# The compressed branch's probability product on 128 rows of the array instead of 64

## The chip, the cores and the metric

The kernel runs on one core of a Trainium2 chip. The metric is the device time of one execution in microseconds (us). The engines are PE (TensorE; its weight loads are listed apart as PEld), DVE (VectorE), ACT (ScalarE), POOL (GpSimd) and SP, which issues the DMAs. The kernel before took 587.68 us, the median of three runs (586.27, 587.68 and 588.92).

## The reference

Two layers of a decoder trunk on 512 tokens of 1024 channels. Each layer projects its input, runs three mixers side by side (retention, sparse attention, a gated linear recurrence), gates their outputs, projects them back and normalises. The change lies in the sparse attention, in the branch over compressed keys and values. Cut to that branch:

```python
kc = compress(kvh(k_c), cmp_pos[0], cmp_w[0])      # 31 compressed keys per group of heads
vc = compress(kvh(v_c), cmp_pos[1], cmp_w[1])      # 31 compressed values, 64 wide
p_c = masked_softmax(einsum('bgrqd,bgnd->bgrqn', qb, kc), m_c)
o_c = einsum('bgrqn,bgnd->bgrqd', p_c, vc)         # the product that is changed
o_s, o_w = ...                                     # selected blocks, sliding window
return gb[..., 0:1] * o_c + gb[..., 1:2] * o_s + gb[..., 2:3] * o_w
```

Two groups of four heads each share keys and values.

## The kernel before, in words

Every float32 product is made of two parts in the type float32r: a rounded high part and the rest as a low part. An operation of the program is not issued when it is written down. It is recorded as an `Op` (`Engine.__getattr__`, all under line 204) with a cost and its dependencies, and `Plan.schedule` then makes one fixed order per engine: a list schedule by the longest path to the end, to which a random number per operation is added (`noise[op.ix]`, 300 ns times a normal draw, `op.ix` being the operation's place in the program), and six rounds of packing backward and forward. `Plan.forward` gives each engine the operation that can start first. So the order on every engine, and which projection products stand between two steps of the attention, come from that plan; at run time the engines only wait on semaphores.

The attention (lines 983 to 990) runs, in each layer, over four tiles of 128 tokens in the order 1, 2, 0, 3 and over two groups. `scores` makes the probabilities, `softmax_cmp` those of the compressed branch (`pcm`, 4 heads by 32 columns). `values` adds all branches up in one PSUM bank `po` (tag `O`, one bank): for the other branches 128-row products of `vst` with the transposed probabilities `th` and `tl` (512 columns each), and at lines 964 to 973 the compressed branch. There `pcm` is transposed into a bank of tag `T`, four ACT copies put the high parts of the four heads on partitions 0 to 31 of `pc`, four DVE subtractions put the low parts on partitions 32 to 63, and one product of 512 columns with the stationary operand `vcs` closes the step. `vcs` holds the compressed values twice, on partitions 0 to 31 and 32 to 63, and their low parts in its second 64 columns; partitions 64 to 127 of both tiles exist and are not used. This product is made 16 times: 2 layers, 4 tiles, 2 groups. I call these the 16 sites.

`pc` has one place (`PCB = 1`), so each use waits until the product before has read it. `vcs` is written once per layer, by four small copies and subtractions at lines 709 to 712, and has one place as well. Projection products (bank tag `A`), retention (tag `M`), transposes (tag `T`) and scores (tag `S`) fill PE between the sites; nearly all of them use 128 rows and 128 columns. POOL works mainly on the low parts of the weights (`wl`), which the products of the next weights wait for.

Of the kernel before, what the change touches and what calls it, by code (L numbers as in the profile page):

```python
# [10 lines left out]
F32 = mybir.dt.float32  # L11
F32R = mybir.dt.float32r
# [5 lines left out]
P = 128  # L18
# [17 lines left out]
# columns of w_in in the order in which they are projected  # L36
# [36 lines left out]
# columns of the table of constants  # L73
# [38 lines left out]
COLD = 6827.0  # the array's clock is halved until then  # L112
TURN = 130.0  # between two engines' accesses to a bank
GRAIN = 8
# [4 lines left out]
PCB = 1  # L119
# how a token tile's halves are normalised: on DVE; on ACT and DVE; on ACT, DVE and Pool  # L120
# [16 lines left out]
class Ref:  # L137
    """A view of a buffer whose place is known once the schedule is."""
# [26 lines left out]
class Slots:  # L165
    """Places of one kind; buffers take them in the order in which they are made."""
# [23 lines left out]
class Engine:  # L190
# [23 lines left out]
    def locks(self, what, args, kw):  # L214
        """Whether an instruction holds the SBUF ports that DVE and Pool share."""
        at = lambda x: x.view(0) if isinstance(x, Ref) else x
        if self.name == "POOL":
            return True
        if self.name != "DVE":
            return False  # L220
        big = [at(x) for x in args[1:] if isinstance(x, Ref) and int(np.prod(at(x).shape[1:])) > 1]
        big += [at(v) for k, v in kw.items() if isinstance(v, Ref) and k not in ("accum_out", "scalar1", "scalar2")]
        sbuf = [x for x in big if x.space != PSUM]
        if len(sbuf) > 1:
            return True
        return what in ("tensor_copy", "tensor_scalar", "memset") and len(sbuf) == len(big) and at(args[0]).space != PSUM

    def together(self, *products):
        """Matrix products that the array takes side by side, as one instruction of the plan."""
        def call():  # L230
            for out, lhsT, rhs, kw in products:
                self.queue.matmul(out.view(), lhsT.view(), rhs.view(), **kw)  # L232

        cost = self.cost("matmul", products[0][:3], {}) + 102.0 * (len(products) - 1)
        self.plan.add(self.name, call, cost, [r for x in products for r in x[1:3]], [x[0] for x in products], None, False)
# [35 lines left out]
class Plan:  # L271
# [7 lines left out]
    def touched(self, ref):  # L279
        """The quarters of the partitions and the cells of GRAIN elements that a view touches, as bits."""  # L280
        ap = ref.view(0)
        key = (tuple(map(tuple, ap.ap)), ap.offset, ap.space == PSUM)
        if key not in self.cells:
            (stride, count), *free = key[0]
            first, at = divmod(ap.offset, stride)
            cells = np.array([at])
            for st, n in free:
                cells = np.unique((cells[:, None] + st * np.arange(n)).ravel())
            if ap.space == PSUM:
                cells = np.arange(512)  # L290
                first, count = 0, P
            rows = sum(1 << q for q in range(first // 32, (first + count - 1) // 32 + 1))
            self.cells[key] = rows, sum(1 << int(c) for c in np.unique(cells // GRAIN))
        return self.cells[key]
# [34 lines left out]
    def schedule(self):  # L329
        """A list schedule by the longest path to the end, then rounds of packing to the end and to the start."""  # L330
        rank, noise = {}, NOISE * np.random.RandomState(SEED).standard_normal(len(self.ops))
        for op in reversed(self.ops):
            rank[op] = op.cost + max((self.lag(op, o) + rank[o] for o in op.before), default=0.0)
        self.end = self.forward({op: noise[op.ix] - rank[op] - op.bias for op in self.ops})
        best = self.end, {op: op.start for op in self.ops}
        for _ in range(ROUNDS):
            self.end = self.forward(self.backward())
            if self.end < best[0]:
                best = self.end, {op: op.start for op in self.ops}
        if best[0] < self.end:  # L340
            self.end = self.forward(best[1])
        return self.end

    def forward(self, prio):
        """Every engine takes what it can start first, the least prio first; the end of the last."""
# [13 lines left out]
        def place(op):  # L359
            """When the buffers that an instruction is the first to touch have places, or None."""  # L360
            t = 0.0
            for b in op.bufs:
                if b.slot is None:
                    if b.pool.next != b.at or not b.pool.free:
                        return None
                    t = max(t, min(b.pool.free)[0])
                t = max([t] + [end + TURN for e, end in b.seen.items() if e != op.eng])
            return t
# [45 lines left out]
    def backward(self):  # L414
        """The latest starts that still end with the last schedule, with its places for the buffers."""
# [19 lines left out]
        start = {}  # L435
# [28 lines left out]
def hybrid_kernel(ctx: ExitStack, tc: tile.TileContext, xt_d, xn_d, w_in_d, w_out_d, gb_d, cmpw_d, cmpp_d, lruw_d,  # L464
# [29 lines left out]
    # products of zeros, which raise the array's clock while the first loads are on their way  # L494
# [5 lines left out]
    # x, later y, transposed, as two float32r parts  # L500
# [8 lines left out]
    # ---------------------------------------------------------------- weights  # L509
# [9 lines left out]
    def weights(l, name):  # L519
        if (l, name) not in parts:  # L520
# [5 lines left out]
            for h in W_HALVES:  # L526
# [4 lines left out]
                if first:  # L531
                    # a slice of the weights and of x at a time
# [23 lines left out]
    def proj_t(w, m, out):  # L556
        """out [128 columns m of the chunk, 512 tokens] = W^T X^T"""
        c = slice(m * P, (m + 1) * P)
        for n, k in enumerate(K_ORDER):
            hi, lo = w[k]  # L560
            T.matmul(out, hi[:, c], XH[:, k, :], start=(n == 0), stop=False)
            T.matmul(out, hi[:, c], XL[:, k, :], start=False, stop=False)
            T.matmul(out, lo[:, c], XH[:, k, :], start=False, stop=(n == KT - 1))

    def proj_n(w, tiles, order=K_ORDER):
        """out [128 tokens of tile i, columns of the chunk] = X W for each (i, out)"""
# [9 lines left out]
    for l in range(DEPTH):  # L576
        last = l == DEPTH - 1
        # ------------------------------------------ values and branch gates
# [19 lines left out]
        # ------------------------------------------ parameters  # L598
# [13 lines left out]
        # log-decay of the LRU: sp = softplus(-lam), c1 = -4 sp, c2 = 2 sp  # L612
# [23 lines left out]
        # ------------------------------------------ keys, two stacked parts  # L636
        # per group and part: the selected keys, last tile first; the compressed keys; the window's keys
# [20 lines left out]
        # ------------------------------------------ queries, two stacked parts  # L658
# [16 lines left out]
        # ------------------------------------------ compressed keys and values  # L675
        vcs = sb([P, 2, 2 * HD], "vcs", dt=F32R)
        w = weights(l, "cmp")
# [9 lines left out]
        # keys and values side by side in the array's columns  # L687
# [4 lines left out]
        for i in range(2):  # L692
# [9 lines left out]
            else:  # L702
                # twice over the partitions, for the two parts of the probabilities
# [11 lines left out]
        # ------------------------------------------ retention  # L715
# [37 lines left out]
        def retention():  # L753
            for n in range(NT):
# [5 lines left out]
                # queries of two heads on the partitions; keys of one head, the other head's rows zero  # L760
# [58 lines left out]
        # ------------------------------------------ RG-LRU  # L819
        def lru():  # L820
# [14 lines left out]
            for c in range(2):  # L835
# [4 lines left out]
                for e in range(2):  # L840
                    # a block's two parts over each other, its two gates side by side
# [29 lines left out]
        # ------------------------------------------ attention  # L871
        def gate_rec(d, i, g, b):
            """d <- 0.25 gate / d"""
# [10 lines left out]
        def softmax(i, g, b, r, ps, p_, d, nmx):  # L884
            """exp(score - max) of one head and branch, and its sum"""
# [6 lines left out]
        def softmax_cmp(i, g, pcm):  # L892
            """the compressed branch's probabilities from its masked scores, four heads"""
# [10 lines left out]
        def scores(i, g, branches):  # L904
            """the scaled probabilities of the branches: 0 selected (tiles in falling order), 1 window"""
# [18 lines left out]
            for r in range(4):  # L924
                tile_ = sb([P, S], "P", PBUFS)
                # columns of kst for each bank, and what lies where in it
# [24 lines left out]
        def values(i, g, probs, pcm, po, first, last):  # L951
# [12 lines left out]
            if pcm is not None:  # L964
                # the high parts over the low parts
                pt = bank("T")
                T.transpose(pt[:, :P], pcm.rearrange("p r n -> p (r n)"), ident)
                pc = sb([P, 4, P], "pc", PCB, F32R)
# [4 lines left out]
                T.matmul(po, vcs[0:64, g, :], pc[0:64].rearrange("p r t -> p (r t)"), start=False, stop=last)  # L973
# [20 lines left out]
        # ------------------------------------------ gates of the NSA output  # L994
# [30 lines left out]
        # ------------------------------------------ output projection, norm  # L1025
# [66 lines left out]
def _layout(inputs):  # L1092
# [14 lines left out]
    # per block of channels: its weights twice over the partitions; columns of the two gates, the block's own half first  # L1107
# [28 lines left out]
```

## Time and profile before

| | before |
|---|---|
| median of 3 runs | 587.68 us (586.27 to 588.92) |
| span of the profiled execution | 586.1 us |
| PE busy | 564.7 us, 96% |
| weight loads (PEld) busy | 498.3 us, 85% |
| DVE / ACT / POOL busy | 71% / 57% / 50% |
| granted TensorE clock, mean | 0.995 of full speed |

The profile is of one execution. For it only the span from the first to the last instruction is known; it lies 0.2 us under the fastest of the three runs and 1.6 us under their median. Matmuls are pipelined and the ends in their rows are modelled, so that neighbouring matmuls overlap in the rows. What one product takes of PE's time is read from start to start, not from its length.

### The profile page before, as it was taken

What the parts mean: (1) busy time and instruction counts of PE and PEld (TensorE: products, weight loads), DVE (VectorE), ACT (ScalarE), POOL (GpSimd) and SP (SyncE); (2) the same over time, 40 slices, a digit from 0 to 9 for tenths busy, and PEclk for the clock granted to TensorE, in tenths of its full rate; (3) what the DMA queues carried; (4) which work ended last, traced back from release to release, by engine and by line L of the source; (5) the groups of instructions that cost most, each with busy time, mean ns of one, the idle gap of its engine ahead of it and who ended that gap; (6) DMA issues with size and microseconds to landing.
All of it is one profiled execution on the core that took longest, in us unless ns stands there. A gap on an engine that the chain in (4) does not pass through costs nothing.

```text
span 586.1 us, 10490 instructions
## 1 busy us (share of the span) xinstructions
PE 564.7 (96%) x3670; PEld 498.3 (85%) x3670; DVE 415.7 (71%) x1237; ACT 336.7 (57%) x785; POOL 294.6 (50%) x349
## 2 busy tenths in 40 slices
PE   8999999999989999999989999999999999999994
PEld 8888867889878888899988888788899888788994
DVE  6663499889998776743793227798797888676247
ACT  6464477698666655722443456758985666564220
POOL 3655155335845255754483454432596514378532
PEclk9999999999999999999999999999999999999997
DMA  8733222110323044343362433120213202332403
GB/s 259 263 100 108 73 72 73 38 36 1 85 61 91 4 124 116 100 148 104 137 180 55 125 79 103 37 73 1 73 38 107 71 21 57 106 127 59 134 7 145
DMA packets 44069, 52.63 MB, mean 90 GB/s; under 512 B 2928, under 2 KB 36720, under 8 KB 44016
## 3 DMA queue, kind: packets, MB, share of 16 engines
q1 hardware_dynamic: 44016, 51.95, 29.8%
q8 instruction: 29, 0.48, 0.3%
q14 instruction: 24, 0.20, 0.1%
HBM read 47.75 MB, written 4.19 MB: 89 GB/s over the span
## 4 chain that ended last, share of the span: by engine, by line
PE 71%; DVE 14%; ACT 8%; issue 2%; DMA 2%; POOL 2%; SPq 0%; DVEq 0%; POOLq 0%; ACTq 0%
PE A L204 50%; PE T L204 6%; PE S L204 6%; PE O L204 4%; PE M L204 4%; DVE P L204 3%; ACT pc L204 2%; DVE pc L204 2%; DVE R L204 2%; ACT P L204 2%; DVE Y L204 2%; DMA wr<-in_w_in_dram 1%; DVE ptl L204 1%; ACT R L204 1%; PE M L232 1%
## 5 line engine op out<-in xcount | busy, mean ns | idle before, releaser
L204 POOL TENSOR_TENSOR wl<-wr,wh 128x512 fp32r<-128x512 f32 (+2 forms) x136 | 180.6, 1343 | 111.5 <-ACT wh L204 93.0
L204 PE MATMUL A<-wh,XL 128*128 128x256 f32 (+1 forms) x560 | 155.3, 288 | 0.7 <-DVE XL L204 0.7
L204 PE MATMUL A<-wh,XH 128*128 128x256 f32 (+1 forms) x560 | 154.1, 288 | 1.1 <-ACT wh L204 1.1
L204 PE MATMUL A<-wl,XH 128*128 128x256 f32 (+1 forms) x560 | 153.6, 285 | 0.0
L204 ACT ACTIVATE wh<-wr 128x512 fp32r<-128x512 f32 (+2 forms) x140 | 82.0, 613 | 65.9 <-PE A L204 40.7
L204 PEld LDWEIGHTS A<-wh,XL 128*128 128x128 f32 x560 | 104.3, 190 | 3.6 <-issue 1.0
L204 PEld LDWEIGHTS A<-wh,XH 128*128 128x128 f32 x560 | 103.6, 189 | 4.0 <-ACT wh L204 1.4
L204 PEld LDWEIGHTS A<-wl,XH 128*128 128x128 f32 x560 | 104.1, 189 | 1.7 <-issue 0.2
L204 PE MATMUL A<-XH,wl 128*128 128x512 f32 x256 | 101.3, 405 | 0.0
L204 PE MATMUL A<-XL,wh 128*128 128x512 f32 x256 | 100.4, 401 | 0.0
L204 PE MATMUL A<-XH,wh 128*128 128x512 f32 x256 | 100.2, 401 | 0.0
L204 ACT ACTIVATE P<-P,nmx 128x128 f32<-128x128 f32 (+3 forms) x128 | 71.0, 556 | 36.4 <-DVE nmx L204 36.0
L204 DVE TENSOR_TENSOR ptl<-T,pth 128x512 fp32r<-128x512 f32 x80 | 55.0, 687 | 26.9 <-ACT pth L204 24.6
L204 ACT ACTIVATE pth<-T 128x512 fp32r<-128x512 f32 x80 | 47.5, 594 | 39.6 <-PE T L204 35.0
L204 DVE CUSTOM_DVE_ANT_0 P<-S,con 128x128 f32<-128x128 f32 (+3 forms) x128 | 60.0, 483 | 12.6 <-PE S L204 9.1
L204 POOL TENSOR_SCALAR P<-P,den 128x256 f32<-128x256 f32 (+3 forms) x64 | 38.9, 619 | 57.8 <-DVE denc L204 22.1
L204 PE MATMUL T<-con,P 128*128 128x128 f32 x320 | 58.5, 276 | 6.3 <-DVE pc L204 2.9
L204 PE MATMUL S<-K,Q 128*128 128x288 f32 (+4 forms) x240 | 61.0, 340 | 1.2 <-DVE nmx L204 1.0
L204 PEld LDWEIGHTS A<-XL,wh 128*128 128x128 f32 x256 | 48.2, 188 | 9.5 <-issue 0.2
L204 PEld LDWEIGHTS A<-XH,wl 128*128 128x128 f32 x256 | 48.2, 189 | 9.4 <-issue 0.9
L204 PEld LDWEIGHTS A<-XH,wh 128*128 128x128 f32 x256 | 48.3, 189 | 9.2 <-issue 0.7
L204 PEld LDWEIGHTS T<-con,P 128*128 128x128 f32 x320 | 39.6, 140 | 18.0 <-issue 4.4
(156 smaller groups left out, 899.4 us busy)
## 6 DMA issues: line engine op xcount, KB each, us to landing
wr<-in_w_in_dram SPq DMA_DIRECT2D x48, 512.0 KB, 3.8
wr<-in_w_out_dram SPq DMA_DIRECT2D x16, 512.0 KB, 3.9
Y<-in_xt_dram SPq DMA_DIRECT2D x8, 256.0 KB, 4.1
Y<-in_cmpw_dram SPq DMA_DIRECT2D x4, 512.0 KB, 6.1
R<-in_xn_dram SPq DMA_DIRECT2D x8, 256.0 KB, 3.4
P<-in_gb_dram SPq DMA_DIRECT2D x8, 256.0 KB, 3.9
x<-R SPq DMA_DIRECT2D x8, 256.0 KB, 2.0
R<-x SPq DMA_DIRECT2D x8, 256.0 KB, 3.1
```

The source lines that it names most:

```text
L204: return f(*[at(x) for x in args], **{k: at(v) for k, v in kw.items()})
L232: self.queue.matmul(out.view(), lhsT.view(), rhs.view(), **kw)
```

## The change

The product runs on all 128 partitions of `vcs` and `pc`. Partitions 64 to 127 of both are filled with zeros by POOL: of `pc` once, near the start of the program, where `pc` becomes one lasting tile in place of a new buffer per use; of `vcs` once per layer, before its values are written. The copies, subtractions and transposes stay as they are. The zeros add nothing to the sums. The three new operations move the place number of every operation behind them by one to three. The rest of the diff takes comments out.

```diff
-PCB = 1
...
     V.memset(kz[:, 0, 1, :], 0.0)
     V.memset(kz[:, 1, :, :], 0.0)
+    pc = sb([P, 4, P], "pc", 1, F32R)
+    G.memset(pc.bitcast(F32)[2 * 32:], 0.0)
...
         vcs = sb([P, 2, 2 * HD], "vcs", dt=F32R)
+        G.memset(vcs.bitcast(F32)[2 * 32:], 0.0)
         w = weights(l, "cmp")
...
                 T.transpose(pt[:, :P], pcm.rearrange("p r n -> p (r n)"), ident)
-                pc = sb([P, 4, P], "pc", PCB, F32R)
                 for r in range(4):
                     A.activation(pc[0:32, r, :], pt[32 * r:32 * r + 32, :P], AF.Copy)
                 for r in range(4):
                     V.tensor_sub(pc[32:64, r, :], pt[32 * r:32 * r + 32, :P], pc.bitcast(F32)[0:32, r, :])
-                T.matmul(po, vcs[0:64, g, :], pc[0:64].rearrange("p r t -> p (r t)"), start=False, stop=last)
+                T.matmul(po, vcs[:, g, :], pc.rearrange("p r t -> p (r t)"), start=False, stop=last)
```

## Rows read from the trace of the kernel before

**Rows 1.** Page, part 1: busy time, share of the span, instructions.

```profile
PE 564.7 (96%) x3670; PEld 498.3 (85%) x3670; DVE 415.7 (71%) x1237; ACT 336.7 (57%) x785; POOL 294.6 (50%) x349
```

**Rows 2.** Page, part 4: the chain that ended last, by engine.

```profile
PE 71%; DVE 14%; ACT 8%; issue 2%; DMA 2%; POOL 2%; SPq 0%; DVEq 0%; POOLq 0%; ACTq 0%
```

**Rows 3.** Stretches: us; PE, PEld, DVE, ACT, POOL busy; clock, DMA share, GB/s.

```profile
91.00:200.00 109.00, 104.90 (x704) 92.55 (x703) 97.39 (x334) 76.11 (x188) 54.06 (x71) 1.00 0.19 52
...
250.00:305.00 55.00, 52.63 (x437) 51.82 (x435) 33.53 (x67) 18.62 (x33) 30.59 (x26) 1.00 0.45 138
...
375.00:480.00 105.00, 102.79 (x692) 91.30 (x692) 91.29 (x307) 77.64 (x196) 54.75 (x74) 1.00 0.20 54
```

**Rows 4.** Tile O: products, lengths in ns (min/median/max), first and last start, form.

```profile
L204 PE MATMUL O<-ptl,vst x80: 388/396/484, 80.0 to 530.5; 128*128 128x512 f32 x80
L204 PE MATMUL O<-pc,vcs x16: 465/492/503, 91.3 to 531.5; 64*128 64x512 f32 x16
```

**Rows 5.** Timeline of PE at a site: start us, length us, instruction, names, rows*columns, operand.

```profile
247.63 0.28 PE L204 MATMUL A<-wh,XH 128*128 128x256 f32 x1
247.84 0.49 PE L204 MATMUL O<-pc,vcs 64*128 64x512 f32 x1
248.26 0.39 PE L204 MATMUL A<-wh,XH 128*128 128x256 f32 x1
248.49 0.28 PE L204 MATMUL A<-wl,XH 128*128 128x256 f32 x1
```

**Rows 6.** Timeline of PE, 128-row products alone, of 256, 256 and 512 columns.

```profile
109.27 0.28 PE L204 MATMUL A<-wl,XH 128*128 128x256 f32 x1
109.39 0.28 PE L204 MATMUL A<-wh,XL 128*128 128x256 f32 x1
109.50 0.39 PE L204 MATMUL A<-XH,wl 128*128 128x512 f32 x1
109.73 0.53 PE L204 MATMUL S<-K,Q 128*128 128x416 f32 x2
```

**Rows 7.** Timeline of the weight loads in the stretches of Rows 6 and 5.

```profile
109.39 0.19 PEld L204 LDWEIGHTS A<-XH,wl 128*128 128x128 f32 x1
...
247.84 0.18 PEld L204 LDWEIGHTS O<-pc,vcs 64*128 64x128 f32 x1
248.26 0.19 PEld L204 LDWEIGHTS A<-wh,XH 128*128 128x128 f32 x1 [0.24 <-issue]
```

**Rows 8.** Timeline of PE: a site after a wait; a 128-row product whose load was late.

```profile
100.23 0.48 PE L204 MATMUL O<-ptl,vst 128*128 128x512 f32 x1
100.54 0.39 PE L204 MATMUL A<-XH,wl 128*128 128x512 f32 x1
...
450.35 0.47 PE L204 MATMUL O<-pc,vcs 64*128 64x512 f32 x1 [0.21 <-DVE pc L204]
...
450.97 0.28 PE L204 MATMUL A<-wl,XH 128*128 128x256 f32 x1
```

**Rows 9.** Chain that ended last, around two sites: start us, us, what.

```profile
133.17 0.71 ACT R L204
...
179.37 0.42 PE O L204
```

**Rows 10.** POOL: its groups (busy us, mean ns); its timeline at the start.

```profile
L204 POOL MEMSET z<- 128x256 f32 x2 | 0.6, 312 | 0.0
...
6.72 0.78 POOL L204 TENSOR_TENSOR wl<-wr,wh 128x280 fp32r<-128x280 f32 x1 [5.35 <-ACT wh L204]
```

**Rows 11.** Chain that ended last, where the layers meet.

```profile
248.40 1.29 POOL wl L204
```

**Rows 12.** Timeline of PE: first site, and first and last site of layer 1.

```profile
91.25 0.47 PE L204 MATMUL O<-pc,vcs 64*128 64x512 f32 x1
...
379.86 0.49 PE L204 MATMUL O<-pc,vcs 64*128 64x512 f32 x1
...
531.47 0.47 PE L204 MATMUL O<-pc,vcs 64*128 64x512 f32 x1 [0.56 <-DVE pc L204]
```

## The prediction, made before the changed kernel was run

> **What bounds the kernel now.** I read the page first. PE is busy for 96% of the span, and the other engines for 71% or less [rows 1]; 71% of the chain that ended last is PE's own work, 14% DVE's and 8% ACT's [rows 2]. So time taken off PE's queue has a fair chance to come off the end, but not everywhere. The view by stretches says where it may not: in the two stretches that hold most of the attention (91 to 200 us, and 375 to 480 us) DVE is busy for 97.39 of 109 us and 91.29 of 105 us, that is 89% and 87% [rows 3]. There PE and DVE are close to each other. The clock is granted in full in these stretches (1.00), so every price below is one of the 2.4 GHz level.
>
> Then I looked at the changed product itself. Its row is 492 ns long in the median where 128-row products of as many columns into the same bank take 396 [rows 4]. These lengths are modelled, so I went on to the order of starts.
>
> **What a site costs now.** In the stretch around 247.84 us a product of 256 columns, the 64-row product and another product of 256 columns start 0.21, 0.42 and 0.23 us before what follows them: 0.86 us for the three [rows 5]. Three 128-row products of 256, 256 and 512 columns in a row take 109.73 - 109.27 = 0.46 us, of which the one of 512 columns takes 0.23 [rows 6]. So a site that waits for no data costs 0.40 us more than its columns do. The excess has three pieces: the product starts about 0.09 us late (0.21 for 0.12), it holds the next one back by 0.19 (0.42 for 0.23), and the one behind that by another 0.11 (0.23 for 0.12). The weight loads tell why: among 128-row products the load for the next product starts together with the current one, as the load at 109.39 us, whose own product starts at 109.50, does with the product that starts at 109.39 [rows 6, 7]; at the site the load onto 64 rows starts only with its own product, and the next load of 128 rows only with the next one, after 0.24 us in which the loads wait for nothing that the profile shows [rows 7]. Loading ahead stops at both borders between 64 and 128 rows. I worked out the same difference at all 13 sites that wait for no data: it is 0.35 to 0.40 us; I take 0.39.
>
> At the other 3 sites (91.25, 450.35 and 531.47 us) the data come last, and PE stands before the product anyway [rows 8, 12]. There the 64-row product and the one behind it take 450.97 - 450.35 = 0.62 us. A 128-row product of 512 columns whose load also came just ahead of it takes 0.31 us to the next start [rows 8]; with 0.12 for the 256 columns that follow that is 0.43. So 0.19 us is saved there, between 0 and the 0.39 of the other sites.
>
> **What the change removes.** With 128 rows in both operands the borders are gone, and the product should look like any other `O` product of 512 columns. Over all sites that is 13 x 0.39 + 3 x 0.19 = 5.6 us of PE's queue. The rest of a site (transpose, four copies, four subtractions) is the same.
>
> Of the 16 sites 13 are on the chain that ended last, with a row as that at 179.37 us; at the other three (133, 248 and 380 us) the chain passes through ACT or DVE at that time, as at 133.17 [rows 9]. On the chain are the three that wait and ten others: 10 x 0.39 + 3 x 0.19 = 4.5 us. Three quarters of these sites (10 of 13) lie in the two stretches in which DVE is nearly as busy as PE. When PE gets there sooner, DVE's work on the scores is what is late next, and part of the gain becomes waiting of PE. I can't read that part off a row. Its bounds are nothing kept (0) and more than the chain (5.6); PE's share of what is engine work in the chain, 71 of 93, is the nearest row, so I keep 0.8 of 4.5: 3.6 us [rows 2].
>
> **What the change adds.** Three zero fills on POOL. The fill of `z`, 256 elements per partition, takes 0.31 us [rows 10]; those of `vcs` have as many, on half the partitions, and the one of `pc` has 512, so 0.3 us each and at most about 0.6 us. The fill of `pc` and the first fill of `vcs` depend on nothing and can go where POOL stands idle for 5.35 us until the first weights are there [rows 10]; they cost nothing, and without that cover 0.9 us ahead of the first `wl`. The second fill of `vcs` may start only when the last site of layer 0 has read `vcs` (247.84 us). POOL takes its work in order, so behind it stand the `wl` parts of the output weights, and just there, at 248.40 us, such a part is on the chain [rows 11]. I put 0.3 us on it; it is 0 if the plan sets it later, and some 0.7 us if POOL also has to wait for the site. No DMA and no SP issue is added or moved. No wait is new at a site: `pc` had one place before, and has one now.
>
> **What the change moves.** The program has three more operations, and each later one gets the random number of a neighbour. So the plan is drawn anew, on all engines. No row shows the new order. The nearest thing to a second draw in the trace is the other layer: the same attention under other numbers takes 247.84 - 91.25 = 156.6 us from the first to the last site in layer 0, and 531.47 - 379.86 = 151.6 us in layer 1 [rows 5, 12]. They differ by 5.0 us, so one layer strays by some 2.5 us from their mean, and two layers together by 2.5 x 1.4 = 3.5 us, either way. I add nothing for it to the forecast, and 3.5 us to the range.
>
> **The sum.** -3.6 for the sites that keep their gain, +0.3 for POOL, 0 for the new order: -3.3 us. The profiled execution's span of 586.1 us is 1.6 us under the median of the runs; from that span the sum gives 582.8, and I carry the difference over to the median: 587.7 - 3.3 = 584.4 us.
>
> **The rivals.**
> *The gain stays on PE.* The sites shrink as said, but in the stretches in which DVE is busy for 87 to 89% PE then waits for scores and for `pc`. For it: DVE and ACT hold 22% of the chain. Against it: PE has other products to put in, and 13 sites are on the chain. What is kept then is that outside these stretches, 3 of 13 sites: 2 x 0.39 + 0.19 = 1.0 us, less 0.3 for POOL: 587.0 us.
>
> *The sites don't shrink.* The product keeps 0.42 us to the next start because a load of weights onto all rows must stand back just as well. Then the time is 587.7 + 0.3 = 588.0 us. Against it speaks that 128-row loads do start beside 128-row products [rows 6, 7].
> The Trainium skill has two rules for this rival on its page "TensorE: Matmul & The Clock Gate": in Part 3, "The mechanism", that a weight load overlaps products in flight only when it goes to other row groups, and under "Why this matters for your kernels" that one product over 32 rows takes the same time as one over 128. By either the sum would lack the 4.5 us. The trace disagrees with both: loads onto the same rows overlap, and the 64-row product takes 0.42 us to the next start where 128 rows take 0.23.
>
> *Slower: the new order costs more than the sites give.* The draw leaves both layers with attention as loose as layer 0's or looser: in the stretch from 91 to 200 us PE would wait longer behind DVE. Layer 1 alone at layer 0's 156.6 us costs 5.0 us; both layers 5.0 us looser cost 10. Against the 3.3 us gained it ends slower from a loss of 3.3 us on, and slower by more than 0.5% from 6.2 us on; 10 gives 594.4 us. For it: the order is made without knowing what a border between row counts costs or how long PE really waits. Against it: it needs nearly twice the 3.5 us.
>
> *Faster by the whole sum.* All 16 sites come off (5.6 us) and the new order gains 2.5: 579.6 us.
>
> **How the numbers follow.** A change of 0.5%, 2.9 us, is about what a measurement of this kernel can tell from no change; that is a time below 584.7 or above 590.6. The forecast, 584.4 with 3.5 us either side for the order, has a chance of 0.55, of which 0.33 lie below 584.7 and 0.22 inside. The whole sum has 0.15 and is faster. The gain that stays on PE has 0.13 and sites that don't shrink 0.05; both lie inside. The slower rival has 0.12, nearly all beyond 0.5%. That makes 0.48 faster, 0.40 the same, 0.12 slower. The range runs from 579.8 (the whole sum, with little from the order) to 589.8 (no gain kept, and 2.1 us from the order); it leaves out most of the slower rival and the edge of the fastest.
>
> **What would show it.** In the changed profile the row of this product should read 128*128 and about 396 ns, the next product should start 0.23 us behind it, and its weight load should begin beside the product before, at some 13 sites. If these rows are as before, the first reason is wrong. If they are right and the time is not, the excess must be in PE's waits for DVE and ACT in the two attention stretches (the gain stays on PE), in POOL around the place where the layers meet, or in a longer way from the first to the last site of a layer (the new order). The prediction is wrong as a whole if a site's 0.39 us is gone and the time is above 590.

## The result, and the profile after

The changed kernel takes 595.1 us (median of 4 runs, 593.62 to 598.29) against 587.27 us for the kernel before beside it: 1.3% slower, ratio 1.0131 with a 95% interval from 1.0097 to 1.0165. That lies above the range of the prediction. Its profiled execution has a span of 592.9 us where before had 586.1: 6.8 us more.

The product itself did what was forecast. The page of after, part 1 and the first line of part 4:

```profile
PE 566.2 (95%) x3670; PEld 499.0 (84%) x3670; DVE 420.7 (71%) x1237; ACT 337.2 (57%) x785; POOL 296.4 (50%) x352
PE 69%; DVE 17%; ACT 9%; issue 2%; POOL 1%; DMA 1%; SPq 0%; DVEq 0%; POOLq 0%; ACTq 0%
```

And the rows of tile `vcs` in after (columns as in [rows 4]):

```profile
L203 PE MATMUL O<-pc,vcs x16: 388/474/482, 86.9 to 532.9; 128*128 128x512 f32 x16
L203 POOL MEMSET vcs<- x2: 306/306/307, 1.4 to 256.0; 64x256 f32 x2
```

Against [rows 1, 2] the chain has moved from PE to DVE and ACT (69, 17 and 9% for 71, 14 and 8). A site of after in the timeline of PE:

```profile
465.49 0.28 PE L203 MATMUL A<-wh,XL 128*128 128x256 f32 x1
465.60 0.39 PE L203 MATMUL O<-pc,vcs 128*128 128x512 f32 x1
465.83 0.28 PE L203 MATMUL A<-wh,XH 128*128 128x256 f32 x1
465.95 0.28 PE L203 MATMUL A<-wl,XH 128*128 128x256 f32 x1
```

The weight loads beside it:

```profile
465.49 0.19 PEld L203 LDWEIGHTS O<-pc,vcs 128*128 128x128 f32 x1
465.61 0.19 PEld L203 LDWEIGHTS A<-wh,XH 128*128 128x128 f32 x1
```

The three products now take 465.95 - 465.49 = 0.46 us, where they took 0.86 [rows 5], and just what three 128-row products take [rows 6]. The load for the site starts together with the product before it, at 465.49.

The length of the row isn't the sign that the prediction took it for: it forecast about 396 ns, and the median is 474. Five of the 16 rows are 388 to 400 ns long. Of the other eleven (468 to 482 ns) eight stand behind a transpose and three start late; there the next product starts 0.31 to 0.32 us behind the site in place of 0.23, and behind a transpose the site itself starts only 0.03 to 0.06 us after it. The comparison of starts in the experiments therefore takes the product before a site, the site and the one behind it together.

So the loss lies elsewhere. I cut both traces at the first and the last site of each layer, since these are the same instructions in both. The view by stretches of after (columns as in [rows 3]):

```profile
0.00:87.00 87.00, 83.53 (x468) 69.94 (x469) 51.96 (x156) 51.77 (x121) 41.67 (x54) 1.00 0.49 147
87.00:245.00 158.00, 152.71 (x979) 133.20 (x978) 132.42 (x434) 107.36 (x258) 78.17 (x102) 1.00 0.23 65
245.00:383.00 138.00, 134.34 (x881) 118.75 (x881) 78.51 (x182) 61.41 (x135) 73.66 (x73) 0.99 0.37 109
383.00:533.00 150.00, 146.50 (x958) 129.13 (x958) 127.64 (x404) 103.40 (x251) 76.09 (x98) 1.00 0.22 63
533.00:593.00 60.00, 49.10 (x390) 47.95 (x390) 30.16 (x65) 13.29 (x23) 26.83 (x27) 0.94 0.26 83
```

The same five of before:

```profile
0.00:91.00 91.00, 87.73 (x483) 74.18 (x483) 57.60 (x154) 52.36 (x122) 42.51 (x54) 1.00 0.46 141
91.00:248.00 157.00, 152.76 (x984) 132.84 (x982) 132.98 (x439) 106.99 (x259) 82.55 (x107) 1.00 0.24 68
248.00:380.00 132.00, 129.63 (x861) 115.66 (x861) 70.89 (x176) 61.26 (x133) 66.31 (x64) 1.00 0.36 107
380.00:531.50 151.50, 148.47 (x962) 129.96 (x962) 126.23 (x409) 104.67 (x255) 77.35 (x100) 1.00 0.24 68
531.50:586.20 54.70, 46.13 (x385) 45.63 (x385) 27.98 (x63) 11.46 (x19) 25.91 (x26) 0.94 0.26 86
```

The two attention stretches together are as long as before (308.0 us for 308.5), although all 16 sites lie in them or at their edges: what the sites give there is lost there again. The stretch between the layers is 6.0 us longer and the one behind the last site 5.3. Part of the first is work that moved: 15 fewer products stand before the first site (468 for 483) and 20 more between the layers (881 for 861). The rest is PE standing still and PE at half clock. PE's idle time (length less PE busy) is 26.8 us in all against 21.5, and 2.3 of these 5.3 us are behind the last site, 1.3 between the layers and 1.5 in the two attention stretches. Longer waits than any of before's in its attention (0.93 us at most) stand at two transposes there:

```profile
138.96 0.33 PE L203 MATMUL T<-con,P 128*128 128x128 f32 x1 [1.62 <-DVE ptl L203]
...
454.26 0.30 PE L203 MATMUL T<-con,P 128*128 128x128 f32 x1 [2.10 <-DVE pc L203]
```

What stands at the ends of the layers, from the timeline of PE in after:

```profile
295.31 0.89 PE L203 MATMUL T<-con,R 128*128 128x128 f32 x4 [1.81 <-DVE XL L203]
...
535.83 0.50 PE L203 MATMUL A<-wh,XH 128*128 128x256 f32 x2 [1.52 <-ACT XH L203]
...
537.47 0.39 PE L203 MATMUL A<-wh,XL 128*128 128x256 f32 x1 [0.68 <-DVE XL L203]
```

And the stretches around these three places, in after:

```profile
289.00:295.60 6.60, 4.79 (x41) 4.56 (x40) 6.55 (x9) 2.48 (x5) 6.60 (x5) 1.00 0.35 109
295.60:299.00 3.40, 3.40 (x17) 3.40 (x16) 2.04 (x4) 0.60 (x1) 1.56 (x3) 0.50 0.82 218
...
532.00:537.90 5.90, 3.70 (x20) 2.60 (x19) 5.07 (x10) 4.98 (x11) 5.90 (x9) 1.00 0.43 133
537.90:541.30 3.40, 3.40 (x18) 3.40 (x17) 2.66 (x3) 1.53 (x3) 3.40 (x4) 0.50 0.00 0
```

At the end of each layer PE waits for `XH` and `XL`, the two parts of what the layer hands on, which ACT and DVE make: at 295 us of the next layer's input, at 536 us of the mixers' output. Right behind these waits the granted clock is 0.50, the 1.2 GHz level, for 3.4 us, in which PE does what it would do in some 1.7 us at the upper level (an estimate: half of the stretch). Before has no such stretch ahead of its last product. It does wait for `XL` at the first of these places, 0.53 us at 298.43 and 1.12 us at 304.43, and its clock is 1.00 there.

### The profile page after: what moved, and what is told of

It is laid out like the page before. It is cut to its first block, busy times and chain, and to the rows that moved or that the text cites. A ratio compares the mean times of both kernels' runs of the same rounds, so it can differ in the third digit from the quotient of the medians.

```text
span 592.9 us, 10481 instructions
## 1 busy us (share of the span) xinstructions
PE 566.2 (95%) x3670; PEld 499.0 (84%) x3670; DVE 420.7 (71%) x1237; ACT 337.2 (57%) x785; POOL 296.4 (50%) x352
## 4 chain that ended last, share of the span: by engine, by line
PE 69%; DVE 17%; ACT 9%; issue 2%; POOL 1%; DMA 1%; SPq 0%; DVEq 0%; POOLq 0%; ACTq 0%
PE A L203 49%; PE T L203 6%; PE S L203 5%; PE O L203 5%; DVE P L203 4%; PE M L203 4%; DVE R L203 3%; ACT P L203 2%; DVE pc L203 2%; ACT pc L203 2%; DVE Y L203 1%; DVE ptl L203 1%; PE M L231 1%; ACT lt L203 1%; ACT pth L203 1%
## 5 line engine op out<-in xcount | busy, mean ns | idle before, releaser
L203 PE MATMUL A<-wh,XH 128*128 128x256 f32 (+1 forms) x560 | 155.9, 288 | 3.4 <-ACT XH L203 1.8
L203 PEld LDWEIGHTS A<-wh,XH 128*128 128x128 f32 x560 | 105.3, 191 | 7.5 <-ACT XH L203 2.3
L203 PE MATMUL A<-XH,wl 128*128 128x512 f32 x256 | 99.1, 398 | 0.0
L203 ACT ACTIVATE P<-P,nmx 128x256 f32<-128x256 f32 (+3 forms) x128 | 70.9, 555 | 26.5 <-DVE nmx L203 26.1
L203 DVE CUSTOM_DVE_ANT_0 P<-S,con 128x256 f32<-128x256 f32 (+3 forms) x128 | 59.7, 483 | 7.5 <-PE S L203 5.1
L203 PE MATMUL T<-con,P 128*128 128x128 f32 x320 | 53.5, 275 | 6.0 <-DVE pc L203 3.1
L203 PEld LDWEIGHTS T<-con,P 128*128 128x128 f32 x320 | 38.1, 140 | 16.7 <-issue 6.9
```

Source lines behind the costliest of these rows:

```text
L203: return f(*[at(x) for x in args], **{k: at(v) for k, v in kw.items()})
```

## The experiments

The question was whether the 128-row product or the new order costs the time, and what is left of the sites' 5.6 us. All kernels compute the plan in the same way, so two kernels can be given the same order on every engine. The plan's own end, which I name below, is the length that the kernel's list schedule works out for itself; it is no measured time, and a border between 64 and 128 rows costs nothing in it.

**The product on 128 rows, in the old order.** Planned as before, issued on 128 rows, zeros filled once ahead of the program:

```diff
-                T.matmul(po, vcs[0:64, g, :], pc[0:64].rearrange("p r t -> p (r t)"), start=False, stop=last)
+                vp, pp = vcs[0:64, g, :], pc[0:64].rearrange("p r t -> p (r t)")
+                vi, pi = vcs[0:128, g, :], pc[0:128].rearrange("p r t -> p (r t)")
+                def product(po=po, vi=vi, pi=pi, last=last):
+                    T.queue.matmul(po.view(), vi.view(), pi.view(), start=False, stop=last)
+                plan.add("PE", product, T.cost("matmul", (po, vp, pp), {}), [vp, pp], [po], None, False)
...
     plan.schedule()
+    for tag in ("pc", "vcs"):
+        nc.gpsimd.memset(kinds[tag].slots[0].bitcast(F32)[2 * 32:], 0.0)
     plan.emit()
```

> Before's plan, every engine's order as before; only the product reads 128 rows, and the two zero fills stand ahead of the program on POOL. Theory 1 (the sites give what was worked out, the new order costs more): 4.5 us less than before, between 3.6 and 5.6, so 582 to 584 us. Rival (the sites' gain becomes waiting on DVE, or 128 rows cost elsewhere): 586 us or more.

Measured: 585.43 us against 587.6, ratio 0.9964 (0.9949 to 0.9978), 2.2 us faster. The direction of theory 1 holds, its size does not; the rival's 586 or more does not hold either. As every engine runs the same list, PE's rows can be laid side by side and each gap between two starts compared. Between the profiled executions the starts at the sites give 4.9 us, and 3.0 us are given back at a dozen other products, 2.0 of it in waits for DVE; 1.1 are lost in a stretch at half clock that before does not have. Another 1.7 us of the difference in span come from the first 20 us, before any site; that is a difference between two executions and not of the edit, since in the two pairs with DVE relieved below the 128-row kernel is the longer one there, by 1.7 and 1.3 us. Sites less give-back, 1.9, is about the measured 2.2. Three of the products at which it is given back, first in before, then in this kernel:

```profile
185.33 0.40 PE L204 MATMUL S<-K,Q 128*128 128x512 f32 x1
185.56 0.28 PE L204 MATMUL T<-con,pcm 128*128 128x128 f32 x1
...
384.51 0.66 PE L204 MATMUL T<-con,P 128*128 128x128 f32 x4 [0.27 <-DVE ptl L204]
...
433.50 0.53 PE L204 MATMUL S<-K,Q 128*128 128x288 f32 x2
```

```profile
183.91 0.40 PE L204 MATMUL S<-K,Q 128*128 128x512 f32 x1
184.56 0.30 PE L204 MATMUL T<-con,pcm 128*128 128x128 f32 x1 [0.26 <-DVE ptl L204]
...
383.62 0.66 PE L204 MATMUL T<-con,P 128*128 128x128 f32 x4 [0.68 <-DVE ptl L204]
...
432.22 0.53 PE L204 MATMUL S<-K,Q 128*128 128x288 f32 x2 [0.49 <-DVE nmx L204]
```

From the start of the product before, the first transpose comes 0.65 us later where it came 0.23 us later; at the second PE waits 0.68 for 0.27 us. Each takes back 0.4 us, one site's gain, and each time PE waits for DVE. Two of the three wait for `ptl`, the last reader of the one bank of tag `T` that the transpose writes.

**The product on 64 rows, in the new order.** After's plan, with 64 rows issued (the same edit the other way round).

> After's plan and order of every engine, zero fills included, but the product reads 64 rows as before. Theory 1: slower than after by what the sites give, 4 to 6 us: 599 to 601 us, some 12 us over before, all of it from the order. Rival (128 rows are what costs the time): at or under 590 us.

Measured: 597.64 us, ratio to before 1.0168 (1.0133 to 1.0203). The product is the same as in before and so are the rows it runs on; the order, with the three fills, costs 10.0 us. Against it the changed kernel (595.1) keeps 2.5 us of the sites, which is not clear of noise (the two intervals overlap; the profiled executions are 3.3 us apart). Side by side their rows give 5.4 us at the sites and 2.6 us given back outside the stretches at half clock.

This kernel has before's product, so it shows where the order costs its time. Its two attention stretches and its three stretches at half clock:

```profile
87.00:246.80 159.80, 155.05 (x979) 134.55 (x977) 132.49 (x434) 107.56 (x258) 77.95 (x102) 0.99 0.23 64
383.20:536.20 153.00, 150.03 (x957) 130.57 (x958) 128.34 (x404) 103.45 (x250) 75.98 (x98) 0.99 0.22 62
...
141.90:145.30 3.40, 3.40 (x16) 2.94 (x14) 2.95 (x20) 2.89 (x11) 1.27 (x3) 0.51 0.43 146
456.00:459.40 3.40, 3.40 (x15) 3.12 (x15) 2.78 (x10) 1.92 (x7) 0.80 (x2) 0.50 0.38 134
541.30:544.70 3.40, 3.40 (x18) 3.40 (x17) 2.59 (x3) 1.32 (x3) 3.40 (x4) 0.50 0.00 0
```

The attention takes 4.3 us more than in before (312.8 for 308.5), the stretch between the layers 4.4 and the one behind the last site 5.3; the stretch ahead of the first site is 4.0 shorter. By kind, PE is idle for 4.0 us more than in before (25.4 for 21.4), and the three stretches at half clock lose some 5.1 (an estimate: half of 3 x 3.4); 1.0 of the 10.1 us between the two profiled executions is left over. The changed kernel has the same order and the same long waits, yet its half clock came at 296 and 538 us, not at 142 and 456: behind which wait the clock falls changed from one execution to the other. (The two kernels differ only in the rows of the 16 products.)

**The whole change with the old random numbers, and before with the new ones.** In the first, the three fills get zero and every other operation the number that it had; in the second, before's program skips three numbers where the fills would stand. The lines that collect the three places in `self.new` are left out here:

```diff
-        rank, noise = {}, NOISE * np.random.RandomState(SEED).standard_normal(len(self.ops))
+        rank, drawn = {}, NOISE * np.random.RandomState(SEED).standard_normal(len(self.ops) - len(self.new))
+        old = [ix for ix in range(len(self.ops)) if ix not in self.new]
+        noise = np.zeros(len(self.ops))
+        noise[old] = drawn
...
```

```diff
-        rank, noise = {}, NOISE * np.random.RandomState(SEED).standard_normal(len(self.ops))
+        rank, drawn = {}, NOISE * np.random.RandomState(SEED).standard_normal(len(self.ops) + len(self.new))
+        noise = [drawn[ix + sum(m <= ix for m in self.new)] for ix in range(len(self.ops))]
...
```

> The whole change, but every operation keeps the random number that it had before; the three new ones get zero. Theory 1a (the shifted random numbers alone spoil the order): back to 582 to 584 us. Theory 1b (the one lasting pc, which ties the 16 sites together in the plan, spoils it): stays at 594 to 596 us. Theory 1c (any small difference gives a new order, and before's was a good one among many): neither, a value between, some 588 to 593 us.

> Before without any of the change, 64 rows, pc with a place per use; only the random numbers are those that the operations get after the change. Theory 1a: as e2, 599 to 601 us. Theory 1b: 587 us, as before. Theory 1c: between, some 590 to 598 us.

Measured: 589.37 us (ratio 1.0024, 1.0010 to 1.0039) and 593.63 us (1.0107, 1.0080 to 1.0134). The order of neither is that of before or of after: with the old numbers the lasting `pc` and the fills alone already give another order. So theories 1a and 1b both fall as sole causes, and 1c stands: each of these small differences in the program gave a new order. Before with nothing of the change in it loses 6.0 us by three skipped numbers. These two runs alone would also allow a sum, 6.0 us for the numbers and 3.9 for the lasting `pc` and the fills (589.37 against 585.43 in the old order, both on 128 rows); the draws below, in which a kernel with both is the fastest, speak against a fixed price of either.

**Other draws.** To see where before stands among such orders, I took the seed alone. Over 120 seeds (0 to 59 and 140 to 199) the plan's own end of before's program is 528.1 in the mean, with a standard deviation of 2.7; the shortest of them, 520.91, is that of seed 174, before's own. For the changed program the same seeds give 527.3 in the mean; seed 174 gives 527.50 and seed 53 the shortest, 519.48.

```diff
-SEED = 174
+SEED = 53
```

> The whole change with another start for the random numbers, 53 in place of 174. Its plan's own end is 519.48, against 527.50 of the changed kernel, 525.56 of the changed kernel with the old numbers and 520.91 of before (units of the plan, in which a site's border costs nothing). Theory O (the order decides, and how long the plan thinks it is says how good it is): on the line of the 128-row kernels measured so far (520.91: 585.4, 525.56: 589.4, 527.50: 595.1) about 583 to 584 us, faster than both kernels. Rival (one lasting pc or the zero fills in the plan cost time of themselves): 590 us or more.

> Before with nothing changed but the start of the random numbers, 175 in place of 174; its plan's own end is 528.32, about the mean of such draws. Theory O: on the line of the 64-row kernels (520.91: 587.6, 524.60: 593.6, 527.50: 597.6) about 598 us, 10 us slower than before. Rival (before is not special, its neighbours are as good): 585 to 591 us.

> The plan and order of the changed kernel under seed 53 (which took 582.6 us), with the product on 64 rows. A third order in which the sites alone are switched. If the part of the 5.6 us that is kept hangs on where PE waits in each order, it lies again near 2 to 3 us: 584.6 to 585.6. Theory F (the full sum is kept in an order with few waits): 588 us.

> The whole change with seed 175, whose plan ends at 527.44, as the changed kernel's own does (527.50). Theory O (its time is what a middling draw gives, nothing is special about the shift by one): 593 to 598 us. Rival (the changed kernel's draw is an unlucky one): 590 us or less.

Measured, all draws together, in order of the plan's own end:

| kernel | rows | plan's own end | measured, us |
|---|---|---|---|
| change, seed 53 | 128 | 519.48 | 582.59 (ratio 0.9912, 0.9889 to 0.9934) |
| its order, 64 rows | 64 | 519.48 | 583.70 (0.9936, 0.9924 to 0.9949) |
| old order, 128 rows | 128 | 520.91 | 585.43 |
| before | 64 | 520.91 | 587.0 to 587.6 |
| before, new numbers | 64 | 524.60 | 593.63 |
| change, old numbers | 128 | 525.56 | 589.37 |
| change, seed 175 | 128 | 527.44 | 592.78 (1.0108, 1.0069 to 1.0148) |
| the change | 128 | 527.50 | 595.1 |
| new order, 64 rows | 64 | 527.50 | 597.64 |
| before, seed 175 | 64 | 528.32 | 604.16 (1.0272, 1.0236 to 1.0307) |

Before's own seed gives the shortest plan of the 120, so before is no middling draw. Within each number of rows the measured time rises with the plan's own end, without an exception. The change with seed 175, whose plan ends where the changed kernel's does, is 5.8 us slower than before; at 592.78 it lies 0.2 us under what theory O had named, and far from the rival. Before under seed 175 was expected at some 598 and took 604. The change with seed 53 is faster than both kernels, and nearly all of that is the order: its product on 64 rows costs only 1.1 us more, less than the 2 to 3 expected and not clear of noise, since the two intervals overlap. The profiled executions show 5.1 us at the sites and 3.9 given back, 1.0 of it at one transpose, while other gaps shrank by 1.1.

**The sites' gain with DVE relieved.** Two pairs in the old order, 64 and 128 rows, from which some of DVE's work is left out: first the low parts of `pc` (these are zeros then), then the low parts `ptl` of the other branches' probabilities. The product is issued as in the old-order kernel above, and what would be unwritten is filled with zeros ahead of the program (both left out of the cuts).

```diff
-                    V.tensor_sub(pc[32:64, r, :], pt[32 * r:32 * r + 32, :P], pc.bitcast(F32)[0:32, r, :])
+                    low = pc[32:64, r, :], pt[32 * r:32 * r + 32, :P], pc.bitcast(F32)[0:32, r, :]
+                    plan.add("DVE", lambda: None, V.cost("tensor_sub", low, {}), list(low[1:]), [low[0]], None,
+                             V.locks("tensor_sub", low, {}))
...
```

> Before's plan and order, 64 rows, but the four subtractions for the low parts of pc are left out at every site (64 of 0.29 us, 18 us of DVE's work; the low parts are zeros then, so the product lacks them). This is the partner of the next run: without them PE waits less for DVE. Theory W (in the old order the sites' gain is given back in waits for DVE): faster than before by 1 to 6 us, 582 to 586 us. Theory N (DVE is not what is late): 587 us.

> The run before with 128 rows. Without the subtractions, theory W says that the sites keep more of their 5.6 us than the 2.2 they kept with them: 3.5 us or more under the partner. Rival (the gain is lost elsewhere, in ACT, PE's half clock or the transposes): again 2 to 2.5 us under the partner.

Measured: 580.46 and 577.28 us, 3.2 us apart. That lies between the two theories. The first of them is 6.7 us under before, more than theory W's 1 to 6. Side by side the rows show 6.2 us at the sites and still 3.0 given back, at the same transposes as above (for instance 0.42 us at `T<-con,pcm`, 0.39 and 0.38 at `T<-con,P`): these wait for `ptl`, which this pair still computes.

```diff
-                split(th, tl, pt)
+                A.activation(th, pt, AF.Copy)
+                low = tl, pt, th.bitcast(F32)
+                plan.add("DVE", lambda: None, V.cost("tensor_sub", low, {}), list(low[1:]), [low[0]], None,
+                         V.locks("tensor_sub", low, {}))
...
```

> Before's order, 64 rows, but the 80 subtractions that make the low parts of the other branches' probabilities (ptl, 0.69 us each, 55 us of DVE's work) are left out; these low parts are zeros. In the run with the old order and 128 rows, PE's lead was given back at transposes that wait for this subtraction, which is the last reader of the one bank of tag T. Partner of the next run. Expected: well under 580 us.

> The run before with 128 rows. Theory W2 (the gain was given back at waits for ptl): without them the sites keep 4 us or more of their 5.6 over the partner. Rival (the gain is lost whatever DVE does, for instance in ACT's copies or at the place where the layers meet): 2 to 3.2 us as in the three pairs before.

Measured: 583.73 and 580.65 us, 3.1 us apart; the partner is also slower than the "well under 580" expected. By the median the 4 us of W2 were missed and the rival's 2 to 3.2 met. The rows say more: 4.9 us at the sites, and only 1.3 us given back where it was 3.0 (without `ptl` there is no wait for it left, and no other transpose took its place). The view of PE's waits, first of the kernel with 128 rows in the old order, then of this 128-row kernel without `ptl` (us in total, times, longest):

```profile
PE T L204 <- DVE pc L204: 2.9, 8, 0.9
PE T L204 <- DVE P L204: 2.6, 4, 0.9
...
PE S L204 <- DVE nmx L204: 1.5, 3, 0.6
...
PE T L204 <- DVE ptl L204: 0.9, 2, 0.7
```

```profile
PE T L204 <- DVE pc L204: 3.1, 8, 0.9
PE T L204 <- DVE P L204: 2.3, 3, 0.9
...
PE S L204 <- DVE nmx L204: 0.7, 2, 0.3
```

The difference between rows and median has one visible candidate: the 128-row kernel ran with a mean granted clock of 0.992 and its partner of 0.994. In the profiled ones the stretch from 162 to 168 us was at 0.72 in the former and at 1.00 in the latter, which cost 1.1 us by the rows. That waits for DVE hold the larger part of what is given back in the old order (2.0 of 3.0 us) is shown row by row; that 4 us would arrive without them, and at an equal clock, is argued only. In the new order waits for DVE and for ACT hold 0.8 us each of the 2.6; the rest stands at gaps for which the rows show no wait.

## Why the prediction was wrong, step by step

*The sites.* Right. The price of 0.39 us and the reading of the loads hold to a hundredth at a single site (0.46 us after, as in [rows 6]), and the sum of 5.6 us is 4.9 to 6.2 in five pairs of traces. The rival in which the sites don't shrink is out. The Trainium skill has, on its page "TensorEngine Tiling (Array Packing)" under "Key Properties", that changing the tiling mode drains the engine; the traces fit that, with 0.39 us there and back, if 64 rows among 128 count as a change of mode, which no run here shows.

*What is kept of them.* Too high: I kept 3.6 us. The old order kept 2.2; the new one kept 2.5 and the order of seed 53 1.1, neither of them clear of noise. The step that was mis-sized here is the factor of 0.8 from the chain's shares [rows 2]. The chain tells what ended last, not how close behind it the others are; at the waits for `ptl` and `nmx` DVE had less than 0.4 us to spare, or was late already. The rival "the gain stays on PE" had the mechanism right and kept too little (1.0).

*POOL.* Too high by 0.3: the fills took 0.52 and 0.31 us as worked out, and the second fill of `vcs` ran at 256 us, ahead of 3.0 us in which POOL was idle.

*The new order.* This is the step that made the forecast wrong. I put 0 on it, with 3.5 us either way, from the length of the attention in the two layers [rows 5, 12]. With the 64-row product it cost 10.0 us. So the prediction's own sign of being wrong as a whole was met: a site's 0.39 us is gone and the time is above 590. Two things were wrong. The measure looked between the first and the last site only and, even there, was too small: the new order takes 4.3 us more in these stretches, some 3.4 of it in two stretches at half clock, and the other 5.7 lie outside them, most of it at the ends of the layers, where PE waits for `XH` and `XL` and then, at one place in this profile, runs at half clock. And the prediction took before for a middling draw, so that a new one could go either way. Before is the shortest of 120 by the plan's own end, 2.7 standard deviations under the mean, and other orders of the same program ran at 593.6 and 604.2 us. A new draw was far more likely to lose than to gain.

*The rival that came true* is "the new order costs more than the sites give", at 594.4 us forecast and 595.1 measured, with a chance of 0.12. That the two agree to 0.7 us is luck. The rival put 10 us on longer waits behind DVE in the attention, 5.0 in each layer; the 64-row kernel lost 4.3 there, more by half clock than by waits, and the rest elsewhere. The rival also took off 3.3 us for the change where 2.5 came.

What stays open is the clock. Why it falls behind one wait and not behind another as long is not shown, and so it is not known how much of the 10.0 us another set of executions of the same order would lose: the four runs of the changed kernel go from 593.62 us at a mean granted clock of 0.991 to 598.29 at 0.982. Half clock is not needed for a loss: the profile of before with the new numbers has none ahead of its last product, and is still 4.5 us longer than before's (590.6 for 586.1), with 3.4 us more idle time of PE.

## What to carry to other kernels

A product on 64 rows among products on 128 costs 0.39 us of PE here, and zeros in the unused rows take that away; but read at each such place how far behind the next engine is, since only 1.1 to 3.2 of the 5.6 us arrived in time, and part of the rest was given back at the waits that came next. Where a kernel's order comes from a schedule with random numbers in it, an edit of the program can draw the order anew, and the draw (20 us between the best and the worst of the 64-row product) can be some nine times what the edit gives in a fixed order (2.2 us). Measure the edit in the old order, and then draw again: of the kernels that leave nothing out, the change with another seed is the fastest here, at 582.6 us, and the same order with 64 rows takes 583.7.

## What was not expected of the hardware

Leaving out 55 us of DVE's work (80 subtractions of 0.69 us) made the kernel only 3.2 us faster (583.73 for 586.96), although DVE is busy for 87 to 89% of the attention. Leaving out only 18 us of it, the low parts of `pc`, gave 6.7 us (580.46 for 587.17): in these two kernels it mattered more which waits the work stood in than how much of it there was. And the granted clock falls to 0.50 for 3.4 us behind short waits in the midst of the kernel: in the changed kernel behind 5.9 us in which PE was busy for 3.7, and behind 6.6 us in which it was busy for 4.8. It does not do so each time: the old order with 128 rows had such a stretch at 163 us in its profile, and before, in the same order, had none.
